# The low half of every third weight chunk made by an accumulating DMA

## The chip, the cores and the metric

The kernel runs on one core of a Trainium2 chip. The metric is the time of one launch in microseconds (us) on the device, the median of several runs. Five engines work side by side, each with its own queue in its own order: PE (TensorE, matrix products into PSUM), DVE (VectorE), ACT (ScalarE), POOL (GpSimd) and SP (SyncE, which here only issues transfers). Transfers run on 16 DMA engines, whoever issues them.

## What is computed

A decoder trunk of two layers over 256 tokens of width 2048, all in float32:

```python
def reference(x, ...):
    for layer in range(DEPTH):                       # 2
        h = rms_norm(x, norm_mix[layer])
        if layer % 2 == 0:
            x = x + swa_ssd_mixer(h, ab_w_in, ..., ab_w_out)   # sliding-window attention and a state-space mixer
        else:
            x = x + dilated_mixer(h, c_w_qkv, ..., c_w_o)      # dilated sliding-window attention
        h = rms_norm(x, norm_ffn[layer])
        x = x + squared_relu_mlp(h, w_up[layer], w_down[layer])  # 2048 -> 8192 -> 2048
    return x
```

Nearly all of the arithmetic is in six products of the activations with weights: `ab_w_in`, `ab_w_out`, `c_w_qkv`, `c_w_o`, and `w_up` and `w_down` of both layers, 416 MB of weights that are each read once.

## The kernel before

**Products in halves.** A product of float32 values is made of three products of the narrower type `float32r`. Each operand is split into a high half `hi` (the value rounded to that type) and a low half `lo` (the value less `hi`), and `hi*hi + hi*lo + lo*hi` is accumulated in PSUM. For activations the halves are made once where they arise. For weights they are made as the weights stream past, and that is where the change is.

**The weight stream.** All products are written as units (`unit`, one block of 512 columns with all its rows), and `run()` cuts them into chunks of two row blocks: `raw`, a tile of 128 partitions by 2 x 512 values, 512 KB. There are 792 chunks. For chunk i, three functions make its operands:

- `fetch(i)` issues the load of `wraw` on SP's queue. There are `RAW` = 4 buffers.
- `high(i)` rounds it on ACT: `whi`, in `AHEAD + 2` = 5 buffers.
- `low(i)` subtracts on DVE: `wlo` = `wraw` - `whi`, in `AHEAD + 1` = 4 buffers.

At step i, before the matmuls of chunk i are written, the loop writes `low(i + 2)`, `fetch(i + 6)` and `high(i + 3)`, so the halves are written two to three chunks ahead of their reader. The order on each engine is the order in which the code writes it; no scheduler moves anything. A write into a buffer waits until the readers of its last content are done.

**Two forms of product.** In a unit with `flip`, the weights are the stationary operand: a chunk has 24 matmuls of 256 columns, in threes (`whi`, `whi`, `wlo`). In the others, activations are stationary and the weights move: 12 matmuls of 512 columns, again in threes (`whi`, `wlo`, `whi`). `w_up` and a part of `ab_w_in` are of the first form, all others of the second.

**Work beside the products.** Norms, attention, the convolution and the state-space scan are generators (`side`). After each row block `tick()` lets some of them write a step, and each step says how many row blocks to wait before the next, so that a result made on ACT or DVE is read by PE some row blocks later.

Chunks 0 to 103 are `ab_w_in`, 104 to 151 `ab_w_out`, 152 to 407 the feed-forward part of layer 0 (units of `w_up` and `w_down` by turns), 408 to 503 `c_w_qkv`, 504 to 535 `c_w_o`, and 536 to 791 the feed-forward part of layer 1.

In the profile every instruction of PE, ACT and DVE has line L71 (the helper that counts them), so the names of tiles tell them apart: `wraw`, `whi` and `wlo` as above, `acc` the PSUM accumulators, `hThi`/`hTlo`, `uh`/`ul`, `mixh`/`mixl` and `oh`/`ol` the halves of activations. The functions with their lines:

Of the kernel before, what the change touches and what calls it, by code (L numbers as in the profile page):

```python
# [8 lines left out]
F32R = mybir.dt.float32r  # L9
I32 = mybir.dt.int32  # L10
AF = mybir.ActivationFunctionType
OP = mybir.AluOpType
# [3 lines left out]
T = 256  # L16
FF = 4 * D
EPS = 1e-5
# [3 lines left out]
KC = 2  # L22
# [9 lines left out]
AHEAD = 3  # L32
# [7 lines left out]
def trunk(ctx: ExitStack, tc: tile.TileContext, x, norm_mix, norm_ffn, w_up, w_down, ab_w_in, ab_q_norm,  # L40
          ab_k_norm, ab_sinks, ab_conv_w, ab_conv_b, ab_dt_bias, ab_a_log, ab_d_skip, ab_gate_norm,
          ab_w_out, c_w_qkv, c_q_norm, c_k_norm, c_w_o, shapes, out):
    nc = tc.nc
    consts = ctx.enter_context(tc.tile_pool(name="consts", bufs=1))
    wpool = ctx.enter_context(tc.tile_pool(name="weights", bufs=4))
# [9 lines left out]
    spent = {"V": 0.0, "S": 0.0, "PE": 0.0}  # L55

    class Engine:
        """an engine whose instructions are charged roughly, so that work beside the products is spread evenly"""

        def __init__(self, engine, name, fixed, each):  # L60
            self.engine, self.name, self.fixed, self.each = engine, name, fixed, each
# [24 lines left out]
    def f32(ap):  # L86
        return ap.bitcast(F32)

    # ---------------------------------------------------------------- constants and parameters
    nc.scalar.preload_act_table(AF.Exp)  # L90
    cst = consts.tile([128, C_ALL], F32, name="cst")
    par0 = w4([32, 128], "par0")
# [51 lines left out]
        V.tensor_copy(cwT, p[:, 128:224])  # L144
        yield 4

    # ---------------------------------------------------------------- work beside the weight stream
    tasks = []
    done = set()
    clock = [0]  # L150

    def side(gen, label=None):
        """a step of gen is emitted between products; it yields how many row blocks to wait before the next"""
        tasks.append([clock[0], gen, label])

    def step(forced=False, skip=()):
# [38 lines left out]
    def free(ps):  # L195
        done.add(id(ps))

    # ---------------------------------------------------------------- small arithmetic
    def rsqrt(v, scale, shape, name):
        """1 / sqrt(v * scale + EPS), from a seed by the exponent and three Newton steps"""  # L200
        a = small.tile(shape, F32, name=name + "a", tag="rs_a")
        y = small.tile(shape, F32, name=name + "y", tag="rs_y")
        t = small.tile(shape, F32, name=name + "t", tag="rs_t")
        V.tensor_scalar(a, v, scale, EPS, op0=OP.mult, op1=OP.add)
        V.tensor_scalar(t.bitcast(I32), a.bitcast(I32), 1, None, op0=OP.logical_shift_right)
        V.tensor_scalar(y.bitcast(I32), t.bitcast(I32), -1.0, float(0x5F3759DF), op0=OP.mult, op1=OP.add)
        for _ in range(3):
            V.tensor_tensor(t, y, y, op=OP.mult)
            V.scalar_tensor_tensor(t, t, -0.5, a, op0=OP.mult, op1=OP.mult)
            V.scalar_tensor_tensor(y, t, 1.5, y, op0=OP.add, op1=OP.mult)  # L210
        return y

    def split(hi, lo, src, gain=None):
        """hi + lo = src (* gain), each of float32r's width"""
        if gain is None:
            S.activation(hi, src, AF.Copy)
            V.tensor_tensor(lo, src, f32(hi), op=OP.subtract)
        else:
            S.activation(hi, src, AF.Copy, scale=gain)
            V.scalar_tensor_tensor(lo, src, gain, f32(hi), op0=OP.mult, op1=OP.subtract)  # L220

    # ---------------------------------------------------------------- products with the weights
    units = []

    def unit(segs, ktiles, after, flip=False, needs={}):
        """rows of tokens by weight columns (flip: weight columns by tokens); ktiles: [(row block, operands)]"""
        units.append((segs, ktiles, after, flip, needs))

    def run():
        todo = [(u, c) for u in units for c in range(0, len(u[1]), KC)]  # L230
        raws, parts = {}, {}
# [13 lines left out]
        def high(i):  # L245
            if i < len(todo):
                raw = raws[i]
                hi = wpool.tile([128, KC, raw.shape[2]], F32R, name="whi", bufs=AHEAD + 2)
                S.activation(hi, raw, AF.Copy)
                parts[i] = [hi]  # L250

        def low(i):
            if i < len(todo):
                raw = raws.pop(i)
                lo = wpool.tile([128, KC, raw.shape[2]], F32R, name="wlo", bufs=AHEAD + 1)
                V.tensor_tensor(lo, raw, f32(parts[i][0]), op=OP.subtract)
                parts[i].append(lo)
# [16 lines left out]
        before = ps = None  # L274
# [45 lines left out]
                pending = after, ps  # L320
        pending[0](pending[1])

    # ---------------------------------------------------------------- the norm of the residual
    class Norm:
        """transposed, gained residual as (hi, lo) blocks; the row factors come after the product"""

        def __init__(self, row, rowwise):
            self.row, self.rowwise = row, rowwise
# [70 lines left out]
        def rsb2(self):  # L399
            return self.rsb[:, None, :].to_broadcast([128, 2, T])  # L400

    # ---------------------------------------------------------------- parts of attention
    def head_norm(nm, ps, n, name):
        """factors of the n heads of 64 columns in ps, the residual's factor included"""
        yield from until(("rs", nm.row))
        sq = w4([128, 2, n * 64], name + "sq")
        for t in range(2):
            S.activation(sq[:, t], ps[t][:, :n * 64], AF.Square, scale=nm.rs_at(t))
        yield 2
        s = small.tile([128, 2, n], F32, name=name + "s", tag="hn_s")  # L410
        V.tensor_reduce(s, sq.rearrange("p t (h e) -> p t h e", e=64), axis=AX.X, op=OP.add)
        y = rsqrt(s, 1.0 / 64, [128, 2, n], name)
        f = small.tile([128, 2, n], F32, name=name + "f", tag="hn_f")
        V.tensor_tensor(f, y, nm.rs[:, :, None].to_broadcast([128, 2, n]), op=OP.mult)
        yield 2
        return f

    def heads_T(nm, ps, gain, name, box):
        """eight heads: norm, then [(two heads, 64), tokens] blocks"""
        f = yield from head_norm(nm, ps, 8, name)  # L420
        qn = w4([128, 2, W], name + "n")
        for t in range(2):
            V.tensor_tensor(qn[:, t].rearrange("p (h e) -> p h e", e=64),
                            ps[t].rearrange("p (h e) -> p h e", e=64),
                            f[:, t, :, None].to_broadcast([128, 8, 64]), op=OP.mult)
        free(ps)
        yield 6
        qT = w4([128, 4, T], name + "T")
        for a in range(2):
            p = aux(name + "p")  # L430
            for b in range(2):
                for t in range(2):
                    PE.transpose(p[:, b * T + t * 128:b * T + (t + 1) * 128],
                                 qn[:, t, (2 * a + b) * 128:(2 * a + b + 1) * 128], ident)
            yield 1
            S.activation(qT[:, 2 * a:2 * a + 2], p.rearrange("p (b t) -> p b t", b=2), AF.Copy,
                         scale=gains[:, gain:gain + 1])
            yield 2
        box.append(qT)
        yield 1  # L440
# [1 line left out]
    BL = ((0, 128), (128, 384))  # L442

    def pair(b, pre, first, qT, kT, vs, hi, lo, mask, mult=None, sink=None, post=None):
        """two heads; blocks (q0,k0) (q1,k0) (q1,k1); kT(b), vs(t, head) pick the keys and values"""
        yield from until(pre)
        if first is not None:
            yield from until(first)
# [63 lines left out]
        split(hi()[:, b], lo()[:, b], o[:, :T])  # L512
        yield 1

    # ---------------------------------------------------------------- the residual's additions
    def add_stripe(ps, j, last=None):
        for t in range(2):
            r = res[:, t, j * W:(j + 1) * W]
# [11 lines left out]

            unit([(w, j * W, W)], ktiles, after, needs=needs if j == 0 else {})

    # ================================================================ layer 0, mixer
    win, wout = ab_w_in[0], ab_w_out[0]
    n0 = Norm(R_MIX, True)
    for j in range(NS):
# [39 lines left out]
        yield 2  # L576

    def steps(ps):
        """dt = softplus(dtx) with log1p(e) = 2 atanh(e / (2 + e)); the decays' prefix sums"""
        st = [128, 2, 32]  # L580
        yield from until(("rs", n0.row))
        V.tensor_scalar(rsh, n0.rs, 0.5, None, op0=OP.mult)
# [79 lines left out]
        unit([(win, AQ + u * W, W)], n0.ktiles(), lambda ps, u=u: swa(u, ps))  # L662

    def conv(ps, ch, y):
        """the causal convolution and 2 * silu of four blocks of channels"""
        pre = w4([128, 4, T], "pre")
        for a in range(2):
            V.tensor_tensor(pre[:, 2 * a:2 * a + 2], ps[a].rearrange("p (b t) -> p b t", b=2), n0.rsb2(), op=OP.mult)
# [40 lines left out]
    dxs, wts = {}, {}  # L709

    def decays(g):
        """(C B^T) * decay of both chunks, for the group's heads, source tokens on the partitions"""
        yield from until("steps")
        wt = []
        for c in range(2):
# [123 lines left out]
    residual_units(wout, [(i, lambda i=i: (mixh[i // 4], mixl[i // 4], i % 4)) for i in range(24)],  # L839
                   {4 * i: ("mix", i) for i in range(6)}, n1)  # L840

    # ================================================================ the feed-forward part
    NB = FF // W

    def mlp(layer, nm, nxt, last=None):
# [43 lines left out]
    n2 = Norm(R_MIX + 16, False)  # L889
    mlp(0, n1, n2)  # L890

    # ================================================================ layer 1, mixer
    wqkv = c_w_qkv[0]
    oh, ol = [None] * 4, [None] * 4

# [64 lines left out]


def _shapes():
    """arrays that follow from the shapes: identity, prefix triangle, masks, branch counts"""
    import numpy as np
    c = np.zeros((128, C_ALL), np.float32)
    i = np.arange(128)
    low = i[:, None] <= i[None, :]
    c[:, C_ID:C_ID + 128] = np.eye(128)
    c[:, C_TRI:C_TRI + 128] = low
    c[:, C_CB:C_CB + 128] = 0.25 * low  # L970
    own = i[:, None] - i[None, :]
    prev = own + 128
    c[:, C_M0:C_M0 + 384] = np.where(np.concatenate([own >= 0, prev <= 127, own >= 0], 1), 0, NEG)
    dist = np.concatenate([own, prev, own], 1)
    n = np.where(dist >= 0, (dist <= 128) + (dist % 4 == 0) * 1 + (dist % 16 == 0) * 1, 0)
    c[:, C_M1:C_M1 + 384] = np.where(n > 0, 0, NEG)
    c[:, C_N1:C_N1 + 384] = n
    return c
# [23 lines left out]
```

## Time and profile before

| | |
|---|---|
| median of 3 runs | 2336.72 us (2336.21 to 2336.78) |
| span of the profiled execution | 2334.6 us |
| PE, busy | 2322.0 us, 14137 matmuls |
| weight loads into PE, busy | 2064.2 us |
| DVE, busy | 1430.6 us, 2188 instructions |
| ACT, busy | 1094.5 us, 1411 instructions |
| POOL, busy | 8.4 us, 20 instructions |
| DMA | 425.09 MB, 182 GB/s over the span |

The span runs from the first to the last instruction of one profiled execution, the time of a run also holds what lies around it. Busy times of engines overlap, so they don't add up to the span. PE's matmuls are pipelined and their ends are modelled: the distance from one start to the next is a better measure of PE's pace than the length of one. In rows of the timeline, the first two numbers are start and length in us, and the bracket at the end tells how long the engine was idle before and what ended that. In rows of groups, the count follows the x, then come total busy time and the mean of one in ns, and behind the bar the idle time ahead of the group and its main releaser. A row of DMA issues gives count, size and median time from issue to landing; a "q" behind an engine's name is its queue.

### The profile page before, as it was taken

The numbers are of one execution on the slowest core, as the hardware profiler recorded it, in microseconds if no ns is written. First come the engines' busy times: TensorE is split into PE (matmuls) and PEld (weight loads), VectorE is DVE, ScalarE is ACT, GpSimd is POOL, SyncE is SP. The second block draws the span as 40 slices with busy tenths as digits, with TensorE's granted clock in tenths as the row PEclk, the third lists the DMA queues.
The fourth block names the chain that finished last, engine by engine and source line by source line (L and its number), as shares of the span: only waits on it lengthen the run. The fifth ranks groups of instructions, "written<-read, shape, count | busy, mean of one in ns | idle before, by whom it ended". The sixth has DMA issues, their size and how long they took to land.

```text
span 2334.6 us, 35702 instructions
## 1 busy us (share of the span) xinstructions
PE 2322.0 (99%) x14137; PEld 2064.2 (88%) x14137; DVE 1430.6 (61%) x2188; ACT 1094.5 (47%) x1411; POOL 8.4 (0%) x20
## 2 busy tenths in 40 slices
PE   8999999999999999999999999999999999999999
PEld 7999988899899899899888778778989989989897
DVE  6779986555555555555566776755555555555554
ACT  5565545444344444444454555554444444344342
POOL 1000000000000000000000000000000000000000
PEclk9999999999999999999999999999999999999999
DMA  7546655565666656656555545456665665656654
GB/s 232 161 144 190 188 164 189 188 183 181 191 189 188 191 184 188 192 187 189 189 180 182 157 152 176 155 165 183 184 191 181 190 191 186 191 185 186 191 188 161
DMA packets 229223, 425.09 MB, mean 182 GB/s; under 512 B 15620, under 2 KB 26160, under 8 KB 229056
## 3 DMA queue, kind: packets, MB, share of 16 engines
q1 hardware_dynamic: 218976, 416.34, 57.7%
q10 hardware_dynamic: 9568, 6.34, 0.9%
q8 instruction: 110, 1.80, 0.3%
q14 instruction: 57, 0.47, 0.1%
q0 software_dynamic: 512, 0.15, 0.0%
HBM read 420.64 MB, written 2.13 MB: 181 GB/s over the span
## 4 chain that ended last, share of the span: by engine, by line
PE 99%; DMA 0%; DVE 0%; ACT 0%; SPq 0%; issue 0%; ACTq 0%
PE acc L71 94%; PE sc L71 1%; PE o L71 1%; PE pT L71 1%; PE yp L71 1%; PE xT L71 1%; DMA wraw<-in_ab_w_in_dram 0%; PE qp L71 0%; PE yo L71 0%; PE kp L71 0%; PE yT L71 0%; PE xtok L71 0%; PE hst L71 0%; DVE wlo L71 0%; ACT whi L71 0%; PE cbp L71 0%
## 5 line engine op out<-in xcount | busy, mean ns | idle before, releaser
L71 DVE TENSOR_TENSOR wlo<-wraw,whi 128x1024 fp32r<-128x1024 f32 (+1 forms) x792 | 962.5, 1218 | 685.1 <-PE acc L71 557.7
L71 ACT ACTIVATE whi<-wraw 128x1024 fp32r<-128x1024 f32 (+1 forms) x792 | 835.8, 1056 | 1085.4 <-PE acc L71 981.9
L71 PE MATMUL acc<-hThi,whi 128*128 128x256 f32 x2432 | 692.5, 285 | 0.0
L71 PE MATMUL acc<-hThi,wlo 128*128 128x256 f32 x2432 | 688.1, 283 | 0.0
L71 PE MATMUL acc<-hTlo,whi 128*128 128x256 f32 x2432 | 688.1, 283 | 0.0
L71 PEld LDWEIGHTS acc<-hThi,whi 128*128 128x128 f32 x2432 | 466.6, 192 | 4.0 <-issue 3.3
L71 PEld LDWEIGHTS acc<-hTlo,whi 128*128 128x128 f32 x2432 | 466.7, 192 | 1.6 <-issue 1.0
L71 PEld LDWEIGHTS acc<-hThi,wlo 128*128 128x128 f32 x2432 | 466.6, 192 | 0.0
L71 PE MATMUL acc<-whi,uh 128*128 128x512 f32 x1024 | 399.1, 390 | 0.0
L71 PE MATMUL acc<-wlo,uh 128*128 128x512 f32 x1024 | 398.5, 389 | 0.0
L71 PE MATMUL acc<-whi,ul 128*128 128x512 f32 x1024 | 398.4, 389 | 0.0
L71 PE MATMUL acc<-whi,hThi 128*128 128x512 f32 (+1 forms) x608 | 243.8, 401 | 2.8 <-ACT hThi L71 2.8
L71 PE MATMUL acc<-whi,hTlo 128*128 128x512 f32 (+1 forms) x608 | 235.9, 388 | 0.3 <-DVE hTlo L71 0.3
L71 PE MATMUL acc<-wlo,hThi 128*128 128x512 f32 (+1 forms) x608 | 235.3, 387 | 0.0
L71 PEld LDWEIGHTS acc<-whi,ul 128*128 128x128 f32 x1024 | 192.2, 188 | 40.1
L71 PEld LDWEIGHTS acc<-whi,uh 128*128 128x128 f32 x1024 | 192.3, 188 | 39.3
L71 PEld LDWEIGHTS acc<-wlo,uh 128*128 128x128 f32 x1024 | 192.3, 188 | 39.2
L71 DVE TENSOR_TENSOR res<-acc,res 128x512 f32<-128x512 f32 x144 | 98.8, 692 | 78.1 <-PE acc L71 78.1
L71 PEld LDWEIGHTS acc<-whi,hThi 128*128 128x128 f32 x608 | 115.4, 190 | 29.5 <-issue 5.9
L71 PEld LDWEIGHTS acc<-whi,hTlo 128*128 128x128 f32 x608 | 115.1, 189 | 24.4 <-DVE hTlo L71 0.9
L71 PEld LDWEIGHTS acc<-wlo,hThi 128*128 128x128 f32 x608 | 115.4, 190 | 21.5 <-issue 1.0
L71 PE MATMUL acc<-whi,mixh 128*128 128x512 f32 x192 | 75.6, 394 | 0.0
(198 smaller groups left out, 1444.5 us busy)
## 6 DMA issues: line engine op xcount, KB each, us to landing
wraw<-in_w_up_dram SPq DMA_DIRECT2D x256, 512.0 KB, 3.7
wraw<-in_w_down_dram SPq DMA_DIRECT2D x256, 512.0 KB, 4.4
wraw<-in_ab_w_in_dram SPq DMA_DIRECT2D x96, 512.0 KB, 3.7
wraw<-in_c_w_qkv_dram SPq DMA_DIRECT2D x96, 512.0 KB, 3.8
wraw<-in_ab_w_out_dram SPq DMA_DIRECT2D x48, 512.0 KB, 3.9
wraw<-in_c_w_o_dram SPq DMA_DIRECT2D x32, 512.0 KB, 3.9
wt<-cumd ACTq DMA_DIRECT2D x8, 512.0 KB, 6.9
res<-in_x_dram SPq DMA_DIRECT2D x4, 512.0 KB, 5.0
```

Source lines behind the costliest of these rows:

```text
L71: return f(out, *a, **k)
```

## The change

For every third chunk from number 33 on, `high(i)` now makes the low half's first part too. ACT writes the negative of `whi` into the `wlo` buffer, and a transfer issued by POOL adds `wraw` onto it in place, so that `wlo` holds `wraw` - `whi` when it lands. `low(i)` does nothing for such a chunk. The name `wlo` and its 4 buffers are shared by both ways.

```diff
     def high(i):
         if i < len(todo):
             raw = raws[i]
             hi = wpool.tile([128, KC, raw.shape[2]], F32R, name="whi", bufs=AHEAD + 2)
             S.activation(hi, raw, AF.Copy)
             parts[i] = [hi]
+            if by_dma(i):
+                lo = wpool.tile([128, KC, raw.shape[2]], F32R, name="wlo", bufs=AHEAD + 1)
+                S.activation(lo, f32(hi), AF.Copy, scale=-1.0)
+                nc.gpsimd.dma_start(lo, raw, accum_op=OP.add)
+                parts[i].append(lo)
+                raws.pop(i)
+
+    def by_dma(i):
+        return i > 32 and i % 3 == 0

     def low(i):
-        if i < len(todo):
+        if i < len(todo) and not by_dma(i):
             raw = raws.pop(i)
```

The diff also drops comment lines and docstrings, which shifts line numbers and nothing else.

On PE no row changes its place. On ACT, in the first feed-forward part, between the steps of one unit (`relu` and `uh`) and the next, before:

```order
L71 ACTIVATE whi<-wraw 128x1024 [waits DMAHW5_49,PE_49]
L71 ACTIVATE whi<-wraw 128x1024 [waits DMAHW6_49,PE_49]
L71 ACTIVATE whi<-wraw 128x1024 [waits DMAHW7_49,PE_49]
L71 ACTIVATE whi<-wraw 128x1024 [waits DMAHW0_49,DVE_49,PE_49]
L71 ACTIVATE whi<-wraw 128x1024 [waits DMAHW1_49,DVE_49,PE_49]
L71 ACTIVATE whi<-wraw 128x1024 [waits DMAHW2_49,DVE_49,PE_49]
L71 ACTIVATE whi<-wraw 128x1024 [waits DMAHW3_49,DVE_49,PE_49]
L71 ACTIVATE whi<-wraw 128x1024 [waits DMAHW4_49,DVE_49,PE_49]
L71 ACTIVATE relu<-relu 128x512 [waits DVE_49]
```

and at the same place in the changed kernel (DMAHW is a load's semaphore, DMASW that of a transfer issued by POOL, the others are the engines'):

```order
L71 ACTIVATE whi<-wraw 128x1024 [waits DMAHW5_49]
L71 ACTIVATE whi<-wraw 128x1024 [waits DMAHW6_49,PE_49]
L71 ACTIVATE whi<-wraw 128x1024 [waits DMAHW7_49,PE_49]
L71 ACTIVATE wlo<-whi 128x1024 [waits DVE_49,DMASW6_49,PE_49,Activation_49]
L71 ACTIVATE whi<-wraw 128x1024 [waits DMAHW0_49]
L71 ACTIVATE whi<-wraw 128x1024 [waits DMAHW1_49,PE_49]
L71 ACTIVATE whi<-wraw 128x1024 [waits DMAHW2_49,DVE_49,PE_49]
L71 ACTIVATE wlo<-whi 128x1024 [waits DVE_49,DMASW7_49,PE_49,Activation_49]
L71 ACTIVATE whi<-wraw 128x1024 [waits DMAHW3_49]
L71 ACTIVATE whi<-wraw 128x1024 [waits DMAHW4_49,PE_49]
L71 ACTIVATE relu<-relu 128x512 [waits DVE_49]
```

Behind each third `whi` stands a `wlo<-whi` with a wait for PE of its own, and the `whi` right after it no longer needs one, since ACT has waited for a later point of PE already.

On SP, a stretch of loads of `w_up` in the same part, before:

```order
L241 DMA wraw<-in_w_up_dram 128x2x512 [waits DMAHW2_49,DVE_49]
L241 DMA wraw<-in_w_up_dram 128x2x512 [waits DMAHW3_49,DVE_49]
L241 DMA wraw<-in_w_up_dram 128x2x512 [waits DMAHW4_49,DVE_49]
L241 DMA wraw<-in_w_up_dram 128x2x512 [waits DMAHW5_49,DVE_49]
L241 DMA wraw<-in_w_up_dram 128x2x512 [waits DMAHW6_49,DVE_49]
L241 DMA wraw<-in_w_up_dram 128x2x512 [waits DMAHW7_49,DVE_49]
```

and there in the changed kernel:

```order
L241 DMA wraw<-in_w_up_dram 128x2x512 [waits DMAHW1_49,DMASW0_49]
L241 DMA wraw<-in_w_up_dram 128x2x512 [waits DMAHW3_49,DVE_49]
L241 DMA wraw<-in_w_up_dram 128x2x512 [waits DMAHW5_49,DVE_49]
L241 DMA wraw<-in_w_up_dram 128x2x512 [waits DMAHW4_49,DMASW1_49]
L241 DMA wraw<-in_w_up_dram 128x2x512 [waits DMAHW6_49,DVE_49]
L241 DMA wraw<-in_w_up_dram 128x2x512 [waits DMAHW0_49,DVE_49]
L241 DMA wraw<-in_w_up_dram 128x2x512 [waits DMAHW7_49,DMASW2_49]
```

Every third load waits for POOL's transfer in the place of DVE, since that transfer is now the last reader of the `wraw` buffer that the load fills.

On POOL, behind the small transfers of the start, 253 rows of one form are new:

```order
L124 DMA dtb<-in_ab_dt_bias_dram 128x32 [waits DMASW4_49]
L124 DMA alog<-in_ab_a_log_dram 128x32 [waits DMASW5_49]
L124 DMA dskip<-in_ab_d_skip_dram 128x32 [waits DMASW6_49]
L124 DMA sinks<-in_ab_sinks_dram 128x16 [waits DMASW7_49]
L254 DMA wlo<-wraw 128x1024 [waits DMAHW1_49,DMASW0_49,Activation_49]
L254 DMA wlo<-wraw 128x1024 [waits DMAHW4_49,DMASW1_49,Activation_49]
L254 DMA wlo<-wraw 128x1024 [waits DMAHW7_49,DMASW2_49,Activation_49]
```

Each waits for its load and for ACT's `wlo<-whi`; POOL has nothing else in its queue by then.

## The prediction

> **What bounds the kernel now.** I read the page's first part for the busiest engine, its chain for what ends the span, and then the waits of that engine.
>
> ```profile
> span 2334.6 us, 35702 instructions
> ...
> PE 2322.0 (99%) x14137; PEld 2064.2 (88%) x14137; DVE 1430.6 (61%) x2188; ACT 1094.5 (47%) x1411; POOL 8.4 (0%) x20
> ...
> PEclk9999999999999999999999999999999999999999
> ...
> PE 99%; DMA 0%; DVE 0%; ACT 0%; SPq 0%; issue 0%; ACTq 0%
> ```
>
> PE is busy in 2322.0 of 2334.6 us, its granted clock is 90% or more in each slice, and 99% of the chain that ends last is PE itself. A change elsewhere can gain at most the 12.6 us left, and VectorE's share of that is smaller still. All of PE's waits by name are these (engine and line, releaser, us in total, times, longest):
>
> ```profile
> PE pp L71 <- DMA cst<-in_shapes_dram: 2.9, 1, 2.9
> PE acc L71 <- ACT hThi L71: 2.8, 2, 2.2
> PE xT L71 <- DMA res<-in_x_dram: 2.3, 1, 2.3
> PE acc L71 <- DVE hTlo L71: 0.3, 1, 0.3
> PE pT L71 <- DVE sm L71: 0.2, 1, 0.2
> ```
>
> VectorE costs PE 0.5 us in the whole run, and never through a `wlo`. The engine that the change relieves is not waited for. What the change can do is make `wlo` late, so the question is how early it is due and how long the new way takes. The next rows are two steady stretches, first one where weights are stationary (24 matmuls to a chunk), then one where they are moving (12 matmuls):
>
> ```profile
> 638.93 1.06 ACT L71 ACTIVATE whi<-wraw 128x1024 fp32r<-128x1024 f32 x1 [1.82 <-PE acc L71]
> 641.61 0.28 PE L71 MATMUL acc<-hThi,wlo 128*128 128x256 f32 x1
> 641.73 0.28 PE L71 MATMUL acc<-hThi,whi 128*128 128x256 f32 x1
> 641.81 1.06 ACT L71 ACTIVATE whi<-wraw 128x1024 fp32r<-128x1024 f32 x1 [1.82 <-PE acc L71]
> 641.99 1.23 DVE L71 TENSOR_TENSOR wlo<-wraw,whi 128x1024 fp32r<-128x1024 f32 x1 [1.66 <-PE acc L71]
> ...
> 700.48 0.39 PE L71 MATMUL acc<-whi,uh 128*128 128x512 f32 x1
> 700.51 1.22 DVE L71 TENSOR_TENSOR wlo<-wraw,whi 128x1024 fp32r<-128x1024 f32 x1 [1.49 <-PE acc L71]
> 700.68 1.06 ACT L71 ACTIVATE whi<-wraw 128x1024 fp32r<-128x1024 f32 x1 [1.66 <-PE acc L71]
> 700.71 0.39 PE L71 MATMUL acc<-wlo,uh 128*128 128x512 f32 x1
> 703.40 1.06 ACT L71 ACTIVATE whi<-wraw 128x1024 fp32r<-128x1024 f32 x1 [1.66 <-PE acc L71]
> ```
>
> ScalarE and VectorE each do one tile per chunk, 2.88 us apart (641.81 - 638.93) in the first stretch and 2.72 us (703.40 - 700.68) in the second; that is PE's time for a chunk. Both sit idle until PE releases a buffer: VectorE starts 0.10 us after the end (641.61 + 0.28) of the last matmul that reads the `wlo` buffer it wants. Four such buffers rotate, so the buffer of chunk j comes free when PE leaves chunk j-4, and PE needs it filled three chunks later.
>
> **The change, part by part.** Chunks 33, 36, ..., 789 change: 253 of 792. By the order of the units, 99 of them are in stationary chunks, 111 in steady moving chunks (down, both output projections) and 43 in the other moving chunks, where attention and gating run beside the products.
>
> ```profile
> L71 DVE TENSOR_TENSOR wlo<-wraw,whi 128x1024 fp32r<-128x1024 f32 (+1 forms) x792 | 962.5, 1218 | 685.1 <-PE acc L71 557.7
> L71 ACT ACTIVATE whi<-wraw 128x1024 fp32r<-128x1024 f32 (+1 forms) x792 | 835.8, 1056 | 1085.4 <-PE acc L71 981.9
> ```
>
> *Removed:* 253 subtractions of 1.218 us, 308 us of VectorE. They lay beside PE, and VectorE idled 557.7 us ahead of such tiles waiting for PE, so the gain is 0; its ceiling is the 0.5 us above.
>
> *Added on ScalarE:* 253 negating copies, which I price as the copy of the same shape: 253 x 1.056 = 267 us. The 981.9 us in which ScalarE waits for PE ahead of `whi` hide them. What the copy moves is worse than what it costs: the copy into `whi` of chunk j may start when PE leaves chunk j-5, the one into `wlo` only when PE leaves j-4, and ScalarE is in order. So on each third chunk it stands for PE a chunk longer, and its other work of that step comes after.
>
> *Added on POOL and the DMA engines:* 253 accumulating transfers of 512 KB, SBUF to SBUF. No row of before shows one. The nearest are these:
>
> ```profile
> q1 hardware_dynamic: 218976, 416.34, 57.7%
> ...
> wraw<-in_w_up_dram SPq DMA_DIRECT2D x256, 512.0 KB, 3.7
> wraw<-in_w_down_dram SPq DMA_DIRECT2D x256, 512.0 KB, 4.4
> ...
> wt<-cumd ACTq DMA_DIRECT2D x8, 512.0 KB, 6.9
> ...
> sinks<-in_ab_sinks_dram POOLq DMA_DIRECT2D x1, 8.0 KB, 4.2
> ...
> L124 POOL DMA_DIRECT2D sinks<-in_ab_sinks_dram x1: 537/537/537, 10.5 to 10.5; - x1
> ...
> DMA to landing us min/median/max: 3.4/3.9/8.4
> ```
>
> Issuing holds POOL 0.54 us, 137 us in all on an engine that is otherwise empty: nothing. One 512 KB pass takes the 16 engines 0.577 x 2334.6 / 792 = 1.70 us. An accumulation reads both `wraw` and `wlo`, so I take two passes, 3.4 us. To this comes the way from POOL's issue to a landing, 4.2 us in the row with the least data. My value for issue to landing is L = 4.2 + 3.4 = 7.6 us. From below, it costs no less than the quickest load, 3.4 us. From above, the 512 KB transfer of small pieces took 6.9 us as a median; a third and fourth pass would give 9.3 and 11.0 us. I choose 7.6 because it is the sum nearest to the POOL row, which alone has the same issuer.
>
> The Trainium skill has a lower price. "DMA: Bandwidth & Descriptors", section "Anatomy of one DMA — SWDGE (gpsimd) path", fits 2.0 us plus bytes / 436 GB/s to a transfer issued by GpSimd, which for 512 KB would be an estimate of 3.2 us and by which the sum below would be nothing. The POOL row disagrees, with 4.2 us for 8 KB, under the crowd of first loads.
>
> *The deadline.* Stationary: three chunks are 8.64 us; PE's first matmul on `wlo` is its third, 0.24 us in (641.73 - 641.61 is one); the copy starts 0.26 us in (641.99 - 641.73) and takes 1.06; two hand-overs at the 0.10 us seen take 0.2. That leaves 8.64 + 0.24 - 0.26 - 1.06 - 0.2 = 7.36 us for L. Moving, where it is the second and the copy can start 0.03 us in: 8.16 + 0.23 - 0.03 - 1.06 - 0.2 = 7.10 us. L of 7.6 is late by 0.24 and 0.50 us, and PE, in order, stands at that matmul. 99 x 0.24 + 111 x 0.50 = 24 + 56 = 80 us. The 43 chunks among attention last longer:
>
> ```profile
> L241 SPq DMA_DIRECT2D wraw<-in_c_w_qkv_dram x96: 367/368/368, 1188.9 to 1482.7; - x96
> ...
> 0.00:30.00 30.00, 21.67 (x127) 20.14 (x128) 15.30 (x30) 20.16 (x44) 8.41 (x20) 0.94 0.87 269
> ```
>
> The 96 loads of `c_w_qkv` start over 293.8 us (first row), 95 steps of 3.09 us each, 9.28 us for three: about 8.2 us for L, not late by themselves.
>
> *What queues behind.* `wraw` of such a chunk comes free when the transfer lands, not after VectorE's 1.22 us. SP's queue is in order, so the load of chunk j+4 and the ones after it stand. With L = 7.6 the buffer frees 9.0 us after PE entered chunk j-3, 0.4 us into chunk j; a load of about 4.4 us, the two copies and the subtraction (1.06 + 1.22) end some 7.2 us into j, and PE needs them at four chunks, 11.5 us. Products are covered by 4 us. But ScalarE stands at that `whi` until the load has come, some 4.9 us into chunk j where it used to start at 0.2, and the attention work queued behind it is late for PE's small matmuls. It costs between nothing and one chunk (3.1 us) at 43 places, 0 to 133 us; I take 0.7 us each, 30 us, nearer to nothing since that work is written one to six row blocks ahead of its reader.
>
> *Engines:* 57.7% plus 253 x 3.4 / 2334.6 = 36.8% is 94.5%: nearly full, which is a reason why L may be longer than I take it.
>
> Sum: 2334.6 + 80 + 30 = 2444.6 of span; the three runs (2336.2 to 2336.8) lie 2.1 us over the span, so about **2447 us**, 4.7% slower.
>
> **The rivals.**
>
> *The transfer is hidden (not slower).* If the second read runs beside the first, one pass, L = 4.2 + 1.7 = 5.9 us, under both limits by over a us. Then PE sees nothing: 2334 to 2341 us. For it: the 4.2 us was taken while first loads crowded the engines. Against it: 94.5% if the engines do work twice. It decides at L = 7.1.
>
> *Three passes or more.* L = 9.3: late by 1.94, 2.20 and, among attention, 1.1 us: 192 + 244 + 47 = 483, 2820 us. Four passes, L = 11.0: 3.64, 3.90 and 2.8 us: 360 + 433 + 120 = 913, 3250 us. For it: the engines would then be asked for more than all their time, and nothing in before shows what an addition costs there.
>
> *VectorE holds up POOL's issue.* If issuing must wait out one VectorE tile of 1.22 us, L = 8.8: late by 1.44, 1.70 and 0.6: 143 + 189 + 26 = 358, 2695 us. POOL's rows show no such wait, but VectorE was nearly idle there. The Trainium skill's "SBUF — State Buffer", section "Who interferes with whom", says that GpSimd writes these transfers' descriptors over ports that VectorE locks in its two-port modes; it also holds that a two-input subtraction lets them write, and no run here shows either.
>
> *The change does not do what it says.* The order shows 253 transfers on POOL and 253 copies on ScalarE, and PE's own order is the same in every row, so I leave this no weight beyond the faster case: PE has 12.6 us to give, 8.3 us of it in the first 30 us (30.00 - 21.67, the window row above), before chunk 33.
>
> **How the numbers follow.** A measurement of this kernel can tell about 0.2%, 4.7 us, from no change. Chances: forecast (L between 7.1 and 8.5, 2341 to 2650) 0.45; hidden 0.22; VectorE in the way 0.05; three passes or more 0.26, of it 0.10 above 2900; faster 0.02. The range 2330 to 2900 leaves out about 0.12, the four passes and the faster tail. Slower 0.75 (0.45 + 0.05 + 0.26, less 0.01 for a forecast that lands within 0.2%), same 0.23, faster 0.02.
>
> **What would show it.** Each step has a row of its own in the changed kernel's profile: the landing of `wlo<-wraw` on POOL's queue (7.6 here; 7.1 decides); PE waiting for that DMA at `acc`, some 210 times by 0.2 to 0.5 us; the DMA share near 0.9; ScalarE's `wlo<-whi` at 1.06 us; SP's loads released by that DMA; PE's waits for ScalarE among attention, 30 us. I am wrong if landing takes under 7 us, and wrong in size if it takes over 9.

## The result, and the profile after

The changed kernel takes 2425.12 us as a median (2418.92 to 2434.07), before takes 2336.47 (2336.10 to 2336.78): 88.7 us more, a ratio of 1.0382 (95% interval 1.0362 to 1.0403). 2447 us was forecast. Of the four runs of the 17-slot control further down, one took 2937.08 us at a granted clock of 0.73 and is left out of that control's 2437.45 us.

The page of the changed kernel, with the lines that answer to those of before (busy time by engine; queues with packets, MB and share of the 16 engines; the chain; groups with busy time, mean ns and idle time ahead; issues with their median landing):

```profile
span 2419.6 us, 36217 instructions
...
PE 2349.3 (97%) x14137; PEld 2067.1 (85%) x14137; DVE 1129.9 (47%) x1935; ACT 1343.1 (56%) x1664; POOL 229.2 (9%) x273
...
q1 hardware_dynamic: 218976, 416.34, 53.4%
q0 software_dynamic: 36944, 132.81, 28.6%
...
PE 77%; DMA 17%; ACT 3%; issue 1%; DVE 1%; SPq 0%; ACTq 0%; POOLq 0%; DVEq 0%
...
L71 ACT ACTIVATE wlo<-whi 128x1024 fp32r<-128x1024 f32 x253 | 268.2, 1060 | 313.1 <-PE acc L71 244.4
...
wlo<-wraw POOLq DMA_DIRECT2D x253, 512.0 KB, 6.2
```

VectorE lost 300.7 us of work and ScalarE gained 248.6, and neither shows in the time. What shows is the chain, now 17% DMA where 99% was PE. The waits of the changed kernel name the transfer (waiting engine and line, releaser, us in total, times, longest):

```profile
PEld acc L71 <- DMA wlo<-wraw: 81.1, 69, 3.2
PE acc L71 <- DMA wlo<-wraw: 55.8, 52, 2.8
...
SPq L241 <- DMA wlo<-wraw: 1152.8, 250, 10.4
SPq L241 <- DVE wlo L71: 635.9, 254, 5.3
```

PE's weight loads and matmuls both wait for it (the two overlap and aren't to be added). SP's queue waits for it too, 250 times: a load stands until an accumulation has let go of `wraw`. That SP stands is not new, since in before it stood as long for VectorE's subtractions; new is what it stands for:

```profile
SPq L241 <- DVE wlo L71: 1866.7, 754, 7.8
```

Where the time sits can be had without those waits, from the distance between the first matmuls of neighbouring chunks. Summed over all 791 distances, after is 84.4 us longer than before, and 83.0 us of that lie in the chunks that the accumulations feed; the two kinds of chunk between them have 0.7 and 0.8. Of the 253, 67 are over 0.1 us longer, by 1.23 us on the mean and 0.94 us as a median. So it is neither a slower pace nor a constant toll: about a quarter of the accumulations come late, by about a us.

The landings of `wlo<-wraw` (its tile's view: shortest, median and longest time from issue to landing, and POOL's issue in ns):

```profile
L254 POOL DMA_DIRECT2D wlo<-wraw x253: 862/872/914, 99.5 to 2397.4; - x127
...
DMA to landing us min/median/max: 4.5/6.2/10.1
```

The median is well inside the limit of 7.1 to 7.4 us that the prediction worked out. It is the upper quarter that is late (7.6 us at the 75th percentile, 8.7 at the 90th). One such case in the timeline of after, rows of SP, POOL, ScalarE and PE (start, length, idle time ahead in brackets):

```profile
1903.15 10.26 SPq L241 DMA_DIRECT2D wraw<-in_w_up_dram  x6
...
1903.65 0.87 POOL L254 DMA_DIRECT2D wlo<-wraw  x1 [8.27 <-ACT wlo L71]
...
1907.43 1.06 ACT L71 ACTIVATE whi<-wraw 128x1024 fp32r<-128x1024 f32 x1 [4.08 <-DMA wraw<-in_w_up_dram]
...
1911.75 0.28 PE L71 MATMUL acc<-hTlo,whi 128*128 128x256 f32 x1
1912.55 0.39 PE L71 MATMUL acc<-hThi,wlo 128*128 128x256 f32 x1 [0.52 <-DMA wlo<-wraw]
```

POOL issues the accumulation at 1903.65 us. Six loads start in the 10.3 us from 1903.15, three of them in the first 1.0 us, while in before a load starts every 2.7 to 2.9 us. ScalarE stands 4.08 us for one of them, and PE stands at its first matmul on `wlo` until 1912.55, 8.9 us after the issue. The crowd of loads is the pattern to keep in mind: of the gaps between the starts of neighbouring loads, 10 are under 1 us in before, 299 in after.

### The profile page after: what moved, and what is told of

Its sections match the earlier page's. It is cut to its first block, busy times and chain, and to the rows that moved or that the text cites. A ratio compares the mean times of both kernels' runs of the same rounds, so it can differ in the third digit from the quotient of the medians.

```text
span 2419.6 us, 36217 instructions
## 1 busy us (share of the span) xinstructions
PE 2349.3 (97%) x14137; PEld 2067.1 (85%) x14137; DVE 1129.9 (47%) x1935; ACT 1343.1 (56%) x1664; POOL 229.2 (9%) x273
## 4 chain that ended last, share of the span: by engine, by line
PE 77%; DMA 17%; ACT 3%; issue 1%; DVE 1%; SPq 0%; ACTq 0%; POOLq 0%; DVEq 0%
PE acc L71 73%; DMA wlo<-wraw 14%; ACT wlo L71 2%; DMA wraw<-in_w_up_dram 1%; DMA wraw<-in_w_down_dram 1%; PE sc L71 1%; PE o L71 1%; ACT whi L71 1%; PE pT L71 1%; PE yp L71 1%; PE xT L71 0%; DMA wraw<-in_ab_w_in_dram 0%; DMA wraw<-in_ab_w_out_dram 0%; DVE wlo L71 0%; DMA wraw<-in_c_w_qkv_dram 0%
## 5 line engine op out<-in xcount | busy, mean ns | idle before, releaser
L71 DVE TENSOR_TENSOR wlo<-wraw,whi 128x1024 fp32r<-128x1024 f32 (+1 forms) x539 | 654.6, 1216 | 889.4 <-PE acc L71 482.2
L71 ACT ACTIVATE wlo<-whi 128x1024 fp32r<-128x1024 f32 x253 | 268.2, 1060 | 313.1 <-PE acc L71 244.4
L71 PE MATMUL acc<-wlo,uh 128*128 128x512 f32 x1024 | 405.1, 396 | 31.7 <-DMA wlo<-wraw 31.3
L254 POOL DMA_DIRECT2D wlo<-wraw x253 | 220.8, 873 | 2166.4 <-ACT wlo L71 2004.7
```

Of the source, the lines that this page charges most:

```text
L71: return f(out, *a, **k)
L254: nc.gpsimd.dma_start(lo, raw, accum_op=OP.add)
```

## The experiments

The first four ask whether the loss is the late landing or the order of things on ScalarE and SP. All times with ratios are against before on the same chip.

| kernel | us | ratio (95% interval) | landing, min/median/max us |
|---|---|---|---|
| changed | 2425.12 | 1.0382 (1.0362 to 1.0403) | 4.5/6.2/10.1 |
| control, 17 slots | 2437.45 | 1.0423 (1.0402 to 1.0444) | median 6.4 |
| five `wlo` buffers | 2443.46 | 1.0455 (1.0439 to 1.047) | 4.5/7.0/11.2 |
| five `wraw` buffers | 2422.35 | 1.0365 (1.0332 to 1.0397) | median 6.2 |
| copy on ScalarE, addition on VectorE | 2337.46 | 1.0004 (0.9995 to 1.0013) | none |
| plain copies, nothing added | 2340.91 | 1.002 (1.001 to 1.0029) | 2.8/3.6/8.2 |
| 64 KB accumulated | 2337.69, one run | | 2.8/2.8/7.4 |
| two loads of three | 2346.48, one run | | 4.5/5.0/9.9 |
| every sixth chunk | 2338.70 | 1.0009 (1.0 to 1.0018) | 4.5/4.7/8.6 |
| both rings longer, 16 slots | 2373.11 | 1.0159 (1.0144 to 1.0174) | 4.5/6.6/11.6 |
| control, 16 slots | 2428.57 | 1.0403 (1.0386 to 1.0421) | 4.5/6.3/10.3 |
| every second chunk | 2651.70 | 1.1363 (1.133 to 1.1395) | 4.5/5.6/9.5 |
| half of each chunk | 2388.28 | 1.0213 (1.0186 to 1.0239) | 3.2/5.9/9.0 |

**Control with 17 slots.** One more weight buffer takes the room of one slot in SBUF (4 KB in each partition), so the control gives up a slot and nothing else changes.

```diff
-    slots = ctx.enter_context(tc.tile_pool(name="slots", bufs=18))
+    slots = ctx.enter_context(tc.tile_pool(name="slots", bufs=17))
```

> The changed kernel with 17 activation slots in place of 18, which frees the room that the next two kernels need. Control: nothing about the weights changes, so both theories give 2418 to 2434 us, the spread of the changed kernel.

2437.45 us, a little over what was expected: some 0.4% beside the changed kernel. The next two are read against this one.

**One more `wlo` buffer.**

```diff
-lo = wpool.tile([128, KC, raw.shape[2]], F32R, name="wlo", bufs=AHEAD + 1)
+lo = wpool.tile([128, KC, raw.shape[2]], F32R, name="wlo", bufs=AHEAD + 2)
```

> As the control, but five wlo buffers in place of four, so that the negative copy may start a chunk (2.7 to 2.9 us) earlier. Theory (the time is lost where the accumulation lands after PE's first matmul on wlo, three chunks after the buffer came free): landings took 6.2 us as a median and 8.7 us at the 90th percentile, and the limit goes from about 7 to about 9.8 us, so nearly all waits go: 2336 to 2345 us. Rival (the time is lost to order: ScalarE's extra copy and the loads that stand behind the held wraw): the copies and the held buffers are still there, so over half of the loss stays: 2380 us or more.

No gain at all: 2443.46 us. My theory missed. ScalarE's waits show where the gain went. This is the control, then the kernel with five `wlo` buffers:

```profile
ACT whi L71 <- DMA wraw<-in_w_down_dram: 239.6, 163, 6.2
ACT whi L71 <- DMA wraw<-in_w_up_dram: 164.4, 119, 4.5
```

```profile
ACT whi L71 <- DMA wraw<-in_w_down_dram: 339.4, 172, 7.7
ACT whi L71 <- DMA wraw<-in_w_up_dram: 283.4, 151, 5.6
```

The negative copy was free to start a chunk earlier, but ScalarE then stood longer for the loads that lead to it: the copy began 2.3 us after its buffer came free as a median, where it was 0.09 in the control. I read this as a second ring, from a landing that frees `wraw` through the next loads to the next accumulation, which holds at nearly the same place; the run with both rings longer tests it.

**One more `wraw` buffer.**

```diff
-raws[i] = raw = wpool.tile([128, KC, sum(s[2] for s in segs)], F32, name="wraw", bufs=RAW)
+raws[i] = raw = wpool.tile([128, KC, sum(s[2] for s in segs)], F32, name="wraw", bufs=RAW + 1)
```

> As the control, but five wraw buffers in place of four, so that a wraw held by an accumulation no longer stops the load behind it. Theory (landing too late): the limit and the landing stay, and only the tenth of the chunks whose negative copy started over 1.4 us late gets that back: 2400 to 2425 us. Rival (order): the loads are early again, and the time goes to 2336 to 2360 us.

2422.35 us, some 15 us under the control and inside what the theory gave. The loads are early again, as the same two rows show, and most of the loss is still there:

```profile
ACT whi L71 <- DMA wraw<-in_w_down_dram: 68.4, 33, 6.2
ACT whi L71 <- DMA wraw<-in_w_up_dram: 36.7, 23, 3.4
```

So loads that stand behind a held `wraw` are not by themselves what PE waits for.

**ScalarE's part alone.**

```diff
                 S.activation(lo, f32(hi), AF.Copy, scale=-1.0)
-                nc.gpsimd.dma_start(lo, raw, accum_op=OP.add)
                 parts[i].append(lo)
-                raws.pop(i)
...
-        if i < len(todo) and not by_dma(i):
+        if i < len(todo) and by_dma(i):
+            V.tensor_tensor(parts[i][1], raws.pop(i), f32(parts[i][1]), op=OP.add)
+        elif i < len(todo):
             raw = raws.pop(i)
```

> The negative copy on ScalarE stays, and VectorE adds wraw onto it, with no accumulating transfer. Theory (landing too late): PE doesn't wait, 2335 to 2341 us. Rival (ScalarE's extra 268 us and its later start are what costs): 2370 us or more.

2337.46 us, no difference from before. The 253 copies, their later start and ScalarE's order cost nothing; all of the loss comes with the transfers.

The next four ask what makes a landing late.

**The addition.**

```diff
-nc.gpsimd.dma_start(lo, raw, accum_op=OP.add)
+nc.gpsimd.dma_start(lo, raw)
```

> The same transfers from wraw to wlo on the same queue, but plain copies: nothing is added, so wlo holds wraw and the output is not the reference's. Theory (an accumulation costs the engines a second read): POOL's queue falls from 28.6% of the engines to about 17%, the landing from a median of 6.2 to about 5 us, and the time to 2336 to 2355 us. Rival (the way through POOL is the long part, adding costs nothing): share and landing stay, 2410 to 2435 us.

2340.91 us and a landing of 3.6 us. The queue's share, with the span it refers to:

```profile
span 2338.0 us, 36217 instructions
...
q0 software_dynamic: 36944, 132.81, 15.8%
```

A copy of 512 KB takes the engines 0.158 x 2338.0 / 253 = 1.46 us, an accumulation 0.286 x 2419.6 / 253 = 2.74 us, 1.87 times as long: nearly two passes, as the prediction took it. "Collectives: The Full Stack" of the Trainium skill, section "The bandwidth ceiling: the fold count and why AG ≠ RS ≠ AR", puts the double price of a ReduceScatter between cores down to its two source reads and not to the addition itself. These two rows agree with the doubling, for an addition inside one core's SBUF; they can't tell the reads from the addition.

**The way without the bulk.**

```diff
-nc.gpsimd.dma_start(lo, raw, accum_op=OP.add)
+nc.gpsimd.dma_start(lo[:, :, :64], raw[:, :, :64], accum_op=OP.add)
```

> Only the first 64 columns of each row block are accumulated, 64 KB in place of 512 KB; the rest of wlo stays the negative of whi, so the output is not the reference's. It measures what a landing takes without the bulk. Theory: about 1.8 us plus a little for small pieces and for loads in between, a median of 2 to 3.2 us. The prediction's step: 4.2 us plus an eighth of 3.4, about 4.6 us. Both: no late landing, 2334 to 2341 us.

2.8 us at the least and as a median, with POOL's issue itself at 1.20 us for twice as many pieces (64 columns of two row blocks are two pieces in each partition, the whole tile is one):

```profile
L254 POOL DMA_DIRECT2D wlo<-wraw x253: 1191/1200/1266, 99.3 to 2316.4; - x127
...
DMA to landing us min/median/max: 2.8/2.8/7.4
```

Together with the shortest full landing, 4.5 us less 2.74 us of engine time, the way costs about 1.8 us, not 4.2 us. That is an estimate: the plain copy's shortest landing gives 2.8 - 1.46 = 1.3 us, and this run, whose transfers took the engines 0.82 us each (8.9% of its span), gives 2.8 - 0.82 = 2.0 us. The prediction's row was taken among the first loads. The time, 2337.69 us, is that of before.

**Fewer loads beside it.**

```diff
     (segs, ktiles, *_), c = todo[i]
+    if i > 36 and i % 3 == 2:
+        raws[i] = raws[i - 1]
+        return
     kt = ktiles[c][0]
```

> Every third load is left out (the chunk two behind an accumulating one uses the wraw of the chunk ahead of it, so its weights are wrong). Theory (a landing is stretched by loads that share the engines): the median landing falls from 6.2 to about 5.4 us, the 90th percentile from 8.7 to 7.5 or less, and the time to under 2375 us. Rival (the spread belongs to the accumulation itself): both stay within 0.3 us, and the time stays over 2400 us.

The landing falls to 5.0 us, its 90th percentile to 6.6, and the time to 2346.48 us, with the same 253 accumulations. Loads in between stretch a landing. How much of the time saved comes from that, this run doesn't show, since it has a second effect: three chunks now take two `wraw` buffers, not three, which changes when a buffer comes free. The changed kernel's trace says the same of the landing. With the loads counted that start from 2.5 us ahead of an accumulation's issue to 3 us behind it, a window of the same length for all, the landing takes 4.95 us as a median with none (27 cases), 5.43 with one (64), 6.71 with two (98) and 7.31 with three (64).

**Half as many accumulations.**

```diff
-    return i > 32 and i % 3 == 0
+    return i > 32 and i % 6 == 0
```

> Every sixth chunk in place of every third, 127 accumulations. Theory (a late landing costs its own lateness, about 84 us / 253 = 0.33 us on the mean, less with fewer transfers on the engines): 20 to 42 us over before, 2356 to 2379 us. Rival (the engines' total share is what counts, and at half the transfers it has room): under 2345 us.

2338.70 us: 126 accumulations cost about 2 us, not 20 to 42. My theory of a loss in proportion to the number missed here too, and the rival held. Between two accumulations there is now time for the loads to spread out again:

```profile
q0 software_dynamic: 18656, 66.21, 15.5%
...
wlo<-wraw POOLq DMA_DIRECT2D x126, 512.0 KB, 4.7
```

This leaves a theory with a loop in it, argued so far and not shown. An accumulation holds `wraw`, so loads pile up on SP's queue and start together once it lands; the crowd shares the engines with the next accumulation, three chunks on, and stretches it. The last four runs were to test that.

**Both rings longer.** Five `wlo` and five `wraw` buffers, with 16 slots.

> Five wlo buffers and five wraw buffers together, paid for with 16 activation slots in place of 18. Theory A (two rings bind at nearly the same place: landing to wlo's reader three chunks on, and landing to the next loads of wraw to the copies that lead the next accumulation; loosening one leaves the other): both are loose now, 2337 to 2360 us. Theory B (the DMA engines, at 82% in the mean, can't deliver more): no number of buffers helps, 2400 us or more, with the DMA share as high as in the control.

> Control for the run with both rings longer: the changed kernel with 16 activation slots and nothing else. Both theories: as the changed kernel and its 17-slot control, 2420 to 2450 us.

2373.11 us against 2428.57 us of its control: 55 of the 92 us over before are gone. Theory B is out, since the engines did deliver more (a share of 84.4% of the span against 82.6%); theory A has the sign and over half of the size, not all. PE's waits for the transfer, control and then the run:

```profile
PE acc L71 <- DMA wlo<-wraw: 61.7, 52, 2.5
```

```profile
PE acc L71 <- DMA wlo<-wraw: 28.4, 26, 3.0
```

The landing itself is no shorter (6.6 us against 6.3). The longer rings bear lateness better; they don't do away with the crowd.

**Every second chunk.**

```diff
-    return i > 32 and i % 3 == 0
+    return i > 32 and i % 2 == 0
```

> Every second chunk from 34 on in place of every third, 379 accumulations. By the engines' own times, two loads of 1.63 us and an accumulation of 2.74 us are 6.0 us to two chunks, which PE does in 5.44 to 5.76. Theory A and B both then have the engines as the bound, at least 148 x 0.24 + 166 x 0.56 = 129 us over before, and more with latency: 2465 to 2700 us, DMA share 0.93 or more. If only the number of late landings counted (84 us x 379 / 253): 2463 us with a share of about 0.92.

2651.70 us, within what the engines' times gave, and far over what the number of late landings would. The shares are less than expected, though, 46.1 + 42.6 + 0.8 = 89.5%:

```profile
span 2652.5 us, 36014 instructions
...
q1 hardware_dynamic: 218976, 416.34, 46.1%
q0 software_dynamic: 55088, 198.88, 42.6%
```

So even here the engines are not full in the mean, and no run shows what idles them. A part of the time is PE's clock (see "What was not expected").

**Half of each chunk.**

```diff
-                S.activation(lo, f32(hi), AF.Copy, scale=-1.0)
-                nc.gpsimd.dma_start(lo, raw, accum_op=OP.add)
+                S.activation(lo[:, 1], f32(hi[:, 1]), AF.Copy, scale=-1.0)
+                nc.gpsimd.dma_start(lo[:, 1], raw[:, 1], accum_op=OP.add)
```

(`low(i)` subtracts `lo[:, 0]` on VectorE and lets go of `raw` after that.)

> In every third chunk only the second row block is made by the negative copy and the accumulation (256 KB); VectorE subtracts the first. The bytes accumulated are those of every sixth chunk, in twice as many transfers. Theory (late landings, set by bytes and by the loads beside them): landing 1.8 + 1.4 us and some contention, about 3.5 us, and PE reads that half later, so nearly nothing is late: 2336 to 2342 us. Rival (each transfer costs by its number, whatever its size): a loss like that of the changed kernel, 2400 us or more.

2388.28 us, between the two and expected by neither (the trace is of the quickest of four runs, 2376.37 us). The bytes are those of every sixth chunk, and that one cost 2 us:

```profile
q0 software_dynamic: 36944, 66.49, 15.6%
...
wlo<-wraw POOLq DMA_DIRECT2D x253, 256.0 KB, 5.9
```

An accumulation of half the size still lands after 5.9 us, and 387 gaps between load starts are under 1 us, more than in the changed kernel. Bytes alone don't set a landing, and neither does the count of transfers; the loop through `wraw` fits both this run and every sixth chunk, with 162 short gaps. Short gaps alone are not the loss, though: the plain copies have 203 of them and the 64 KB accumulations 230, at nearly the time of before, and both rings longer still have 274 where the control has 300. If it is the crowd, it does harm only beside a transfer that is long itself. The loop fits, but I took no run in which the loads alone were spread out and all else stayed, so how much of the loss is the loop's and how much the engines' load of 82% is open. Open too is why half a chunk crowds the loads more than a whole one.

## Why the prediction was right

*What bounds the kernel, and the gain:* right. Taking 300 us from VectorE gained nothing: the plain copies and the 64 KB accumulations leave its subtractions out too (VectorE is busy 1132.5 and 1133.7 us in them), and took 2340.91 and 2337.69 us.

*ScalarE's copy:* right, 1.060 us each where 1.056 was taken, and hidden.

*The deadline:* right in kind. PE waits at its first matmul on `wlo`, and nowhere else that costs. The hand-over from ScalarE to POOL was 0.29 us, not 0.10, so that the limits were 7.2 and 6.9 us.

*Issue to landing, L = 4.2 + 3.4 = 7.6 us:* both terms were too large. Two passes were right and took 2.74 us, which brought the engines to 82% and not to 94.5%; the way took some 1.8 us. What was missing is the loads in between, from nothing to over 5 us, which I named only as a reason why L may be longer. The median came to 6.2 us, below the 7.1 to 8.5 us on which the forecast rested, and by the prediction's own sign, wrong if landing takes under 7 us, this step failed.

*The sum:* one L for all chunks put 210 of them late by 0.24 to 0.50 us. In fact 67 were late, by 1.23 us on the mean: 16 of the 99 stationary chunks, 46 of the 111 steady moving ones and 5 of the 43 among attention. By kind of chunk, from the distances between first matmuls:

| chunks | forecast, us | measured, us |
|---|---|---|
| stationary, 99 | 24 | 16.9 |
| steady moving, 111 | 56 | 63.2 |
| among attention, 43 | 30 | 2.9 |
| all | 110 | 83.0 |

The first two agree since a mean L above the limit and a spread of L across it gave a like sum here; that is luck, as a median under the limit would have cost nothing by the prediction's way of adding. The third is the term that was mis-sized: I let ScalarE's late `whi` make attention late for PE. ScalarE did stand for loads, but PE's waits for ScalarE grew by 0.6 us in the whole run, from 2.8 to 3.4. A chunk there takes 3.09 us; that this slack was enough is how I read it, and no run tests it.

*The rivals.* A hidden transfer is what the plain copy comes to, one pass, 3.6 us and 4.4 us of loss. Three passes or more are out, by the ratio of 1.87. VectorE in POOL's way is out as well: POOL's issue took 862 to 914 ns with VectorE 47% busy, and a wait for a VectorE tile of 1.2 us would stand out. The Trainium skill's "SBUF — State Buffer", section "Who interferes with whom", lets two-input subtractions pass, as an inference of its own; the trace agrees.

## What to carry to other kernels

Work taken off an engine that nobody waits for gains nothing, however long it took; ask first what the replacement holds and when it lets go. A transfer that sits between two stages of a ring needs its lead measured against the slow quarter of its landings, not the median; here it also lengthened the hold on the buffers at both its ends. When a ring binds, look for the next one: one more buffer on either side alone gained 0.6% or nothing here, both together 2.4% (of before's time, each against its control).

## What was not expected

The loss is far from linear in the number of accumulations: about 2 us for 126, 89 us for 253 and 315 us for 379.

POOL's issue is longer for an accumulation, 0.87 us against 0.53 for a copy of the same shape (the copy's view below), and it goes up with the number of pieces, not with bytes: 1.20 us for 256 pieces of 64 KB in all, 0.87 us for 128 pieces whether they hold 512 KB or, in the run with half of each chunk, 256 KB.

```profile
L254 POOL DMA_DIRECT2D wlo<-wraw x253: 527/527/555, 98.9 to 2318.5; - x127
...
DMA to landing us min/median/max: 2.8/3.6/8.2
```

The Trainium skill's "DMA: Bandwidth & Descriptors" gave 3.2 us for 512 KB issued by GpSimd, an estimate by its section "Anatomy of one DMA — SWDGE (gpsimd) path"; the copy's 2.8 us at its quickest and 3.6 us as a median lie on either side of that, and the accumulation's 4.5 us at its quickest lie over it.

PE's clock takes a part of the loss. In the trace of the changed kernel the granted clock falls to a half five times between the first 30 us and the end, for 3.4 us each, 0.4 to 1.4 us after the end of a wait of 1.8 to 2.8 us for an accumulation. Before has no such stretch there. One of the five, from 892.7 to 896.1 us, with a row of the clock at its normal pace behind it:

```profile
892.06 0.50 PE L71 MATMUL acc<-wlo,uh 128*128 128x512 f32 x1 [1.93 <-DMA wlo<-wraw]
...
893.81 0.63 PE L71 MATMUL acc<-whi,uh 128*128 128x512 f32 x1
894.24 0.63 PE L71 MATMUL acc<-wlo,uh 128*128 128x512 f32 x1
...
896.73 0.39 PE L71 MATMUL acc<-whi,ul 128*128 128x512 f32 x1
896.96 0.39 PE L71 MATMUL acc<-whi,uh 128*128 128x512 f32 x1
```

The starts are 0.43 us apart in it and 0.23 us behind it. By the granted clock each stretch loses 1.7 us, the five together 8.5 of the 83 us, and the stretches of the run with every second chunk lose 65 of its 315 us. In the trace of every sixth chunk there is one late chunk, by 3.9 us, a wait of 2.1 us with such a stretch behind it. A long wait doesn't always bring one: waits of 2.2 and 2.8 us in the changed kernel's trace went without. What decides is not shown.
